# Hybrid encoder layer on one core: branch B's copies of h tied to the projections, its outputs in DRAM by halves of 512 tokens, the low parts of h's sums on VectorE, and branch A's scores of the prompt in runs of four blocks

## The chip, the cores and the metric

One core of a Trainium2 chip runs the whole kernel. The metric is the device time of one execution in microseconds (us); times of single instructions are also in us unless marked ns. The engines are called as in the profile: PE (TensorE, matmuls), PEld (its weight loads), DVE (VectorE), ACT (ScalarE), POOL (GpSimd) and SP (SyncE, which issues all DMAs of this kernel).

## The reference

One encoder layer with shared weights is applied to two batches, a prompt of 512 tokens and a sample of 1024, each of width 1024. All is fp32. Cut to what matters:

```
h = rmsnorm(x, norm_g)
qa, ka, va, za, qb, kb, vb, zb, ga, gb = split(h @ w_in)
oa = neighbourhood_attention(rmsnorm(qa), rmsnorm(ka), va, rpb) * silu(za)   # 8 heads of 64
ob = window_gqa_attention(rmsnorm(qb), rmsnorm(kb), vb, t5, sink) * silu(zb) # 8 heads, 2 of k and v
merged = sigmoid(ga) * (oa @ w_o_a) + sigmoid(gb) * (ob @ w_o_b)
y = x + merged @ w_out
```

Branch A sees the tokens as a grid 64 wide and attends to a window of 8 rows by 16 columns. Branch B attends to tokens at most 128 away; four query heads share one head of k and v.

## The kernel before, in words

Every fp32 matrix is held as two parts, hi and lo, and a product of two matrices is three matmuls: hi·hi, lo·hi and hi·lo. So h lives as `hh` and `hl`, a weight as `whi` and `wlo`, and so on. `split` (L1168) makes the parts of a tile: hi by a rounding copy on ACT (L1172), lo as the difference on DVE or POOL (L1177).

Each batch goes through two phases.

**Attention** (`attention_phase`, L651) works on six groups: A0 to A3 with two heads each, then B0 and B1 with four query heads each. In a group, each tile of 128 tokens is projected (`project`, 24 matmuls at L764 into one of two PSUM banks tagged p). The norm of q and k follows: squares (ACT L783), their sums `ss` (DVE L788), `rs_v` and its power `rs_r` (POOL L795 and L802), and the scaled `qk` (DVE L819), which PE transposes (L864). When the tiles that a block of queries needs are there, `attend` (L911) issues its scores: matmuls with half the rows (L937), for two heads side by side in the array, three for each head, into PSUM banks tagged x (there are five). `weigh` (L961) takes a block's scores on: bias and minimum on DVE (L972), exponential on ACT (L981), the reciprocal of the sums (DVE L1005), scaling on POOL (L1011) or DVE (L1013), transposes on PE (L1029), split of the result `pp` (ACT L1035, DVE L1040), products with v (L1066), and the output `ot` is stored to DRAM by SP (A: L1090, B: L1102). In the prompt the blocks of branch A are taken two at a time, each head with a bank of its own. Between these, "fill" products of the later gate projections use bank d.

Branch B reads h with its tokens in another order, so `project` first copies tiles of `hh` and `hl` into `hb` (L665 on ACT, L667 on DVE). A copy may start once its part of h is there.

**The dense phase** (`dense_phase`, L1139) computes the paths z and g, the merge and the output. Pairs of weight blocks go through one level of Strassen's scheme (`pair_strassen`, L1349), which wants sums S of weight blocks (L1166) and sums T of blocks of h. The sample's four sums T are kept in DRAM, `t_d`, and read back by `stored_sums` (L1236, loads L1245), each in four tiles that are split; their buffers on the way are called U, fh and w. Weights arrive as `raw` (L1257), and `weight_tiles` (L1260) splits them. The matmuls are L1293 to L1295. `post_z` (L1524) takes a finished z tile: it loads the attention output (`ot<-o_d`, L1535; for branch B two loads, even and odd heads, which DVE adds as `ot<-ot`), multiplies (`C<-C,ot`), and stores to `u_d` (L1520).

**The order.** No order is written down by hand. `Flow` (L141 on) plans the whole program before it is built: each operation has a priority, the engines that may do it with a cost on each, and what it must follow. An operation with two engines goes to the one that the plan has free earlier; a rule named `port` keeps two such operations from standing on DVE and POOL at once. Each engine then runs its own list in order. So a change of one operation can move others on all engines.

Of the kernel before, what the change touches and what calls it, by code (L numbers as in the profile page):

```python
# [25 lines left out]
FILL_P, FILL_S = 3, 8  # L26
SLACK = 1.1
SCRATCH = 1024
CLASSIC_P = (4, 8, 4)
# [325 lines left out]
def encoder_kernel(  # L355
# [47 lines left out]
    t_d = dpool.tile([4, 4, P, NT_S // 2], F32, tag="t_d", name="t_d")  # L403
    o_d = {geo.nt: dpool.tile([2, 8, P, geo.nt], F32, tag=f"o_d{geo.nt}", name=f"o_d{geo.nt}") for geo in (gp, gs)}

# [245 lines left out]
    def attention_phase(geo, hh, hl, h_ops, mask_d, early, late):  # L651
# [79 lines left out]
        def project(br, w, t, prio):  # L731
# [179 lines left out]
        def attend(br, gi, g, batch, nb_t, info, prio):  # L911

            nh = 2 if br == "A" else 4
            k0 = 2 * (gi % 2)
            states = []
            for block in batch:
                sums = tuple(tile_([P, 4], F32, tag, 3) for tag in ("mx", "sm", "rs", "es"))
                pss = [bank("x") for _ in range(nh)]
                sbs = [tile_([P, GW], F32, "sb", 8 if nt == NT_S else 9) for _ in range(nh)]
                states.append((block, sums, pss, sbs))  # L920
# [5 lines left out]
            def emit(e):  # L926

                for block, _, pss, _ in states:
                    runs, tiles, width, step, whole = places(block)
                    q = queries(block)  # L930
                    for pair in range(nh // 2):
                        at = runs[0][0] if whole else pair * P
                        for n, (u, k) in enumerate(((0, 0), (0, 1), (1, 0))):
                            for i in range(2):
                                rows = slice(64 * i, 64 * i + 64)
                                kv = kt.t[rows, k0 + k].rearrange("p (t n) -> p t n", n=P)
                                pe.matmul(  # L937
                                    pss[2 * pair + i].t[:, :width], q.t[rows, u, at : at + P],
                                    kv[:, tiles[0] : tiles[-1] + 1 : step], start=n == 0, stop=n == 2,
                                )  # L940

            def queries(block):
# [4 lines left out]
            o = f.op(  # L947
                (("pe", ns),), emit, prio, new=[v for _, _, pss, sbs in states for v in (*pss, *sbs)],
                use=[queries(block) for block in batch], after=[o for b in batch for t in b[1] for o in info[t][2]],
# [11 lines left out]
        def weigh(br, gi, g, block, sums, pss, sbs, nb_t, info, prio):  # L961
# [6 lines left out]

            def score(i, ps, sb):
                def emit(e, i=i, ps=ps, sb=sb):  # L970
                    init = 3.0e38 if br == "A" else nsink[:, 4 * g + i : 4 * g + i + 1]
                    dve.tensor_tensor_reduce(  # L972
                        out=sb.t[:, :width], in0=ps.t[:, :width], in1=bias_of(br, nb_t, i, table), scale=1.0,
                        scalar=init, op0=ALU.add, op1=ALU.min, accum_out=mx.t[:, i : i + 1],
# [16 lines left out]

            for i, (ps, sb) in enumerate(zip(pss, sbs)):
                score(i, ps, sb)
            if br == "B":
# [81 lines left out]
            if br == "A":  # L1076
# [10 lines left out]
                def emit():  # L1087
                    if len(runs) == 1:
                        dst = over(o_d[nt][0, g], runs).rearrange("(i p) n -> p i n", i=2)
                        nc.sync.dma_start(dst, ot.t[:64, ::2])  # L1090
                        return
                    for i in range(2):
                        dst = over(o_d[nt][0, g, 64 * i : 64 * i + 64], runs)
                        nc.sync.dma_start(dst, ot.t[:64, 2 * i].rearrange("p (a b) -> p a b", b=64))

                stores[g, runs[0][0] // 512].append(sp(emit, 65536, prio, use=[ot]))
            else:
                for e in range(2):
                    dst = o_d[nt][e, 4 + 2 * g : 6 + 2 * g, :, runs[0][0] : runs[0][0] + P]
                    dst = dst.rearrange("c (i d) n -> d (c i) n", d=64)  # L1100
                    o = sp(
                        lambda e=e, dst=dst: nc.sync.dma_start(dst, ot.t[e * 64 : e * 64 + 64]),  # L1102
                        131072, prio, use=[ot],
                    )
                    for c in (4 + 2 * g, 5 + 2 * g):
                        for n in range(nt // 512):
                            stores[c, n].append(o)

        f.slack = SLACK
        groups = [("A", 0), ("A", 1), ("A", 2), ("A", 3), ("B", 0), ("B", 1)]  # L1110
        for gi, (br, g) in enumerate(groups):
# [14 lines left out]
            for t in range(nb):  # L1126
# [12 lines left out]
    def dense_phase(geo, hh, hl, h_ops, o_stores, exps_done, start, opened, tp, up, p0, p1, p2, x_t, y_t, classic, fill, after_gates=None, side=None):  # L1139
# [27 lines left out]

        def split(hi, lo, src, n, prio, new_hi, new_lo, src_v, after=()):  # L1168

# [5 lines left out]
            b = f.op(  # L1175
                any_tt(n),
                lambda e: engines[e].tensor_tensor(lo(), src(), hi().bitcast(F32), op=ALU.subtract), prio,  # L1177
# [58 lines left out]
        def stored_sums(prio, d, after):  # L1236

            tv, ops = {}, {}
            for j in (1, 2, 0, 3):
                tv[j] = tuple(f.value(tp, [P, 4, nh], F32R, "T", 8) for _ in range(2))  # L1240
                vh, vl = tv[j]
                for k in range(4):
# [6 lines left out]
                        lambda vh=vh, k=k: vh.t[:, k], lambda vl=vl, k=k: vl.t[:, k], lambda st=st: st.t[:, :nh], nh, prio,  # L1249
                        (vh, k == 0), (vl, k == 0), [st],  # L1250
                    )
# [7 lines left out]

        def weight_tiles(operands, per, prio):  # L1260

# [4 lines left out]
            for i, src in enumerate(operands):  # L1266
                at, q = [], 0
                while q < 4:
# [6 lines left out]
                        lambda src=src, sc=sc: src.t[:, sc], m * P, prio,  # L1275
                        (hi, ti not in seen), (lo, ti not in seen), [src],
                    )
# [71 lines left out]
        def pair_strassen(srcs, post, prio, mov_h, mov_t, seed=None, last=False, kept=None):  # L1349
# [10 lines left out]
            first = [] if kept else [raw[0, 0], raw[0, 1]]  # L1360
            w = weight_tiles([*first, s2, s3, s1, raw[1, 1], s4], 6, prio - 0.5)
            w = [None] * (7 - len(w)) + w
# [161 lines left out]
        def post_z(c, a, n, v, in_psum, prio):  # L1524
# [3 lines left out]
            for e, ot in enumerate(ots):  # L1528
                if c < 4:
                    src, dst = o_d[nt][e, c, :, a : a + n], lambda ot=ot: ot.t[:, :n]  # L1530
                else:
                    src = o_d[nt][e, c].rearrange("p (i n) -> p i n", n=P)[:, :, a // nb : a // nb + m]
                    dst = lambda ot=ot: ot.t[:, :n].rearrange("p (i n) -> p i n", n=m)
                dma(
                    lambda dst=dst, src=src: nc.sync.dma_start(dst(), src), 512 * n, prio - 0.5, new=[ot],  # L1535
                    after=o_stores[c, a // nh],
# [417 lines left out]
```

## Time and profile before

| | us |
|---|---|
| median of three runs | 1136.02 |
| lowest and highest run | 1134.59, 1136.24 |
| the profiled execution | 1135.29 |
| its span | 1133.5 |
| PE busy in it | 1119.0 |

The page and the views tell of one profiled execution, 1135.29 us, of which 1133.5 us are the span from the first to the last instruction. PE's granted clock was 1.00. The stages, by the windows view: the prompt's attention runs from about 30 to 220 us, its dense phase to 404, the sample's attention to about 797 and its dense phase to the end. In that view PE is busy for all of 30 to 404; it lacks 2.6 us of 161 in 404 to 565, 0.2 of 232 in 565 to 797, 2.5 of 31 in 797 to 828, and 2.7 of 305 after that. A row of a timeline reads: start, duration, engine, line and operation, output<-inputs, shapes, how many; in brackets the idle time before it and what ended that. The durations of matmuls are modelled and overlap, so PE's pace is read from start to start.

### The profile page before, as it was taken

What the parts mean: (1) busy time and instruction counts of PE and PEld (TensorE: products, weight loads), DVE (VectorE), ACT (ScalarE), POOL (GpSimd) and SP (SyncE); (2) the same over time, 40 slices, a digit from 0 to 9 for tenths busy, and PEclk for the clock granted to TensorE, in tenths of its full rate; (3) what the DMA queues carried; (4) which work ended last, traced back from release to release, by engine and by line L of the source; (5) the groups of instructions that cost most, each with busy time, mean ns of one, the idle gap of its engine ahead of it and who ended that gap; (6) DMA issues with size and microseconds to landing.
All of it is one profiled execution on the core that took longest, in us unless ns stands there. A gap on an engine that the chain in (4) does not pass through costs nothing.

```text
span 1133.5 us, 18690 instructions
## 1 busy us (share of the span) xinstructions
PE 1119.0 (99%) x6079; PEld 973.2 (86%) x6079; DVE 860.1 (76%) x1988; ACT 651.9 (58%) x1499; POOL 337.3 (30%) x438
## 2 busy tenths in 40 slices
PE   8999999999999999999999999999999999999998
PEld 6999988888888889999999988988788888888887
DVE  5888797587776568787878888885988766677764
ACT  6777987644432257565769888876543335423430
POOL 4653433000011154434324344420333322222211
PEclk9999999999999999999999999999999999999999
DMA  7854543488886732121212314244977645867862
GB/s 263 276 155 138 184 115 103 110 257 248 256 278 216 254 128 91 27 63 30 82 41 85 81 38 112 57 131 121 307 241 234 224 156 170 281 207 222 280 215 93
DMA packets 139108, 186.11 MB, mean 164 GB/s; under 512 B 29897, under 2 KB 68561, under 8 KB 139010
## 3 DMA queue, kind: packets, MB, share of 16 engines
q1 hardware_dynamic: 139010, 184.91, 51.8%
q8 instruction: 48, 0.79, 0.3%
q14 instruction: 50, 0.41, 0.1%
HBM read 137.66 MB, written 51.92 MB: 167 GB/s over the span
## 4 chain that ended last, share of the span: by engine, by line
PE 93%; DMA 2%; DVE 2%; issue 1%; ACT 1%; POOL 1%; SPq 0%; DVEq 0%; ACTq 0%
PE p L764 25%; PE x L1294 9%; PE x L1295 9%; PE x L1293 9%; PE x L1066 5%; PE x L937 5%; PE x L1029 5%; PE d L1293 4%; PE d L1295 4%; PE d L1294 4%; PE p L1294 4%; PE p L1295 4%; PE p L1293 4%; PE x L864 2%; DMA w<-in_w_att_dram 1%
## 5 line engine op out<-in xcount | busy, mean ns | idle before, releaser
L764 PE MATMUL p<-whi,hh 128*128 128x384 f32 x384 | 133.4, 348 | 0.0
L764 PE MATMUL p<-whi,hl 128*128 128x384 f32 x384 | 132.2, 344 | 0.0
L764 PE MATMUL p<-wlo,hh 128*128 128x384 f32 x384 | 131.8, 343 | 0.0
L1172 ACT ACTIVATE whi<-raw 128x512 fp32r<-128x512 f32 (+1 forms) x140 | 81.4, 600 | 71.2 <-PE x L1294 22.3
L981 ACT ACTIVATE sb<-sb,mx 128x384 f32<-128x384 f32 (+1 forms) x192 | 107.8, 565 | 16.9 <-DVE mx L972 16.5
L1295 PE MATMUL x<-T,wlo 128*128 128x512 f32 x280 | 108.9, 389 | 0.0
L1294 PE MATMUL x<-T,whi 128*128 128x512 f32 x280 | 108.9, 389 | 0.0
L1293 PE MATMUL x<-T,whi 128*128 128x512 f32 x280 | 108.9, 389 | 0.0
L764 PE MATMUL p<-whi,hb 128*128 128x384 f32 x384 | 107.6, 346 | 0.0
L1177 POOL TENSOR_TENSOR wlo<-raw,whi 128x512 fp32r<-128x512 f32 (+1 forms) x33 | 39.5, 1204 | 215.6 <-DMA raw<-in_w_g_dram 112.9
L1040 DVE TENSOR_TENSOR pp<-x,pp 128x512 fp32r<-128x512 f32 (+1 forms) x136 | 82.5, 638 | 19.6 <-ACT pp L1035 19.0
L1177 DVE TENSOR_TENSOR wlo<-raw,whi 128x512 fp32r<-128x512 f32 (+1 forms) x107 | 72.0, 682 | 32.3 <-ACT whi L1172 28.7
L802 POOL TENSOR_TENSOR rs_r<-rs_v,mhalf 128x4 f32<-128x4 f32 (+1 forms) x72 | 80.5, 1118 | 5.7
L1035 ACT ACTIVATE pp<-x 128x512 fp32r<-128x512 f32 (+1 forms) x136 | 70.8, 559 | 15.8 <-PE x L1029 14.3
L1294 PE MATMUL x<-hl,whi 128*128 128x512 f32 x200 | 77.8, 389 | 0.0
L1295 PE MATMUL x<-hh,wlo 128*128 128x512 f32 x200 | 77.8, 389 | 0.0
L1293 PE MATMUL x<-hh,whi 128*128 128x512 f32 x200 | 77.8, 389 | 0.0
L1066 PE MATMUL x<-pp,v 128*128 128x256 f32 (+1 forms) x368 | 75.8, 322 | 0.0
L764 PEld LDWEIGHTS p<-whi,hl 128*128 128x128 f32 x384 | 72.6, 189 | 1.3 <-issue 1.0
L764 PEld LDWEIGHTS p<-wlo,hh 128*128 128x128 f32 x384 | 72.7, 189 | 1.0 <-issue 0.7
L764 PEld LDWEIGHTS p<-whi,hh 128*128 128x128 f32 x384 | 72.7, 189 | 0.7 <-DVE v L812 0.3
L764 PEld LDWEIGHTS p<-whi,hb 128*128 128x128 f32 x384 | 69.1, 188 | 3.1 <-issue 1.3
(388 smaller groups left out, 2965.1 us busy)
## 6 DMA issues: line engine op xcount, KB each, us to landing
raw<-in_w_g_dram SPq DMA_DIRECT2D x84, 256.0 KB
w<-in_w_att_dram SPq DMA_DIRECT2D x46, 384.0 KB
raw<-in_w_z_dram SPq DMA_DIRECT2D x40, 256.0 KB
ot<-o_d SPq DMA_DIRECT2D x36, 256.0 KB
g_d<-C SPq DMA_DIRECT2D x34, 256.0 KB
fr<-in_w_g_dram SPq DMA_DIRECT2D x28, 256.0 KB
raw<-in_w_out_dram SPq DMA_DIRECT2D x28, 256.0 KB
out_dram<-C SPq DMA_DIRECT2D x19, 256.0 KB
```

The lines of the kernel that those rows point to most:

```text
L764: pe.matmul(ps.t[:, :GW], part[u](k), mv.t[:, c], start=k == 0 and m == 0, stop=k == KC - 1 and m == 2,)
L802: lambda e: nc.gpsimd.tensor_tensor(r.t[:, :nn], rv.t[:, :nn], mhalf[:, :nn], op=ALU.pow),
L937: pe.matmul(pss[2 * pair + i].t[:, :width], q.t[rows, u, at : at + P], kv[:, tiles[0] : tiles[-1] + 1 : step], start=n == 0, stop=n == 2,)
L981: act.activation(sb.t[:, :width], sb.t[:, :width], AF.Exp, bias=mx.t[:, i : i + 1], scale=-1.0, accum_out=sm.t[:, i : i + 1],)
L1035: lambda e, pt=pt, pp=pp, nn=nn: act.activation(pp.t[:, 0, :nn], pt.t[:, :nn], AF.Copy),
L1040: lambda e, pt=pt, pp=pp, nn=nn: dve.tensor_tensor(pp.t[:, 1, :nn], pt.t[:, :nn], pp.t[:, 0, :nn].bitcast(F32), op=ALU.subtract),
L1066: pe.matmul(out(), v.t[:, vs], mv(), start=first, stop=last)
L1172: (("act", ACT_(n)),), lambda e: act.activation(hi(), src(), AF.Copy), prio,
L1177: lambda e: engines[e].tensor_tensor(lo(), src(), hi().bitcast(F32), op=ALU.subtract), prio,
L1293: pe.matmul(out, hi.t[:, cs], mh(), start=first and k == 0, stop=False, **more)
L1294: pe.matmul(out, hi.t[:, cs], ml(), start=False, stop=False, **more)
L1295: pe.matmul(out, lo.t[:, cs], mh(), start=False, stop=last and k == len(ws) - 1, **more)
```

## The change

There are four edits.

1. A branch B copy now also waits until the projection of six tiles earlier has begun (`AHEAD = 6`; `f.begun` holds the first operation of each projection).
2. Branch B's outputs have a DRAM tensor of their own, `ob_d`, by halves of 512 tokens, with the tokens in the order in which branch B makes them. A sample block's output was stored by two DMAs in pieces of 512 B (one for the even and one for the odd heads); now by two, one for each half, in pieces of 256 B. A prompt block needs one DMA instead of two. `post_z` read branch B's part as 8 pieces of 256 B on each of 128 partitions (sample); now as one line of 2 KB on each.
3. `split` has a new argument `both`. The low parts of the sums T from `t_d`, and of the weight tiles of pair 0, can be made on DVE only; POOL is no longer offered.
4. In the prompt's branch A four blocks go through `attend` together, and two blocks share a PSUM bank: the second writes its scores from column 256 on.

```
+AHEAD = 6
...
-    o_d = {geo.nt: dpool.tile([2, 8, P, geo.nt], ...
+    o_d = {geo.nt: dpool.tile([4, P, geo.nt], ...
+    ob_d = {geo.nt: dpool.tile([geo.nt // 512, 8, P, 512], ...
...
-    prio - 1, new=[hb[m][q]], hold=[v], after=[o for u in h_ops.values() for o in u], port=True,
+    prio - 1, new=[hb[m][q]], hold=[v], port=True,
+    after=[*(o for u in h_ops.values() for o in u), f.begun[nt, prio - AHEAD]],
...
+    shared = br == "A" and nt == NT_P
...
-    pss = [bank("x") for _ in range(nh)]
+    second = shared and len(states) % 2
+    pss = [(v, 256) for v, _ in states[-1][2]] if second else [(bank("x"), 0) for _ in range(nh)]
...
-    for e in range(2):
-        dst = o_d[nt][e, 4 + 2 * g : 6 + 2 * g, :, runs[0][0] : runs[0][0] + P]
-        dst = dst.rearrange("c (i d) n -> d (c i) n", d=64)
+    m, t = 512 // nb, runs[0][0] // P
+    for n in range(nt // 512):
+        dst = ob_d[nt][n, 4 * g : 4 * g + 4, :, t * m : t * m + m].rearrange("a p m -> p a m")
...
-    size = 2 if br == "A" else 1
+    size = 1 if br == "B" else 4 if nt == NT_P else 2
...
-    any_tt(n),
+    any_tt(n)[: 1 + both],
...
+    (vh, k == 0), (vl, k == 0), [st], both=d is m_d,
...
+    w = weight_tiles([*first, s2, s3, s1, raw[1, 1], s4], 6, prio - 0.5, prio > 0)
...
-    src = o_d[nt][e, c].rearrange("p (i n) -> p i n", n=P)[:, :, a // nb : a // nb + m]
+    src = ob_d[nt][a // nh, 2 * c - 8 : 2 * c - 6, e * 64 : e * 64 + 64, :n]
```

The planner makes a new order of it. Three places follow, first the program of before, then the changed one; lines of the changed file are 2 to 6 higher. PE's matmuls are as many as before; in the prompt's attention their order is new, from 220 to 564 us it is the same, and in the sample it differs only near 564 to 646 and 797 to 828.

The first place is the first scores of the prompt's branch A. On PE, before (`kt` and `qt` are the transposed k and q, `d` a fill bank):

```order
L1294 MATMUL d<-hl,fh 128x512
L1295 MATMUL d<-hh,fl 128x512
L764 MATMUL p<-wlo,hh 128x384
L937 MATMUL x<-kt,qt 128x256 x12
L864 MATMUL x<-ident,qk 128x128 x2
L764 MATMUL p<-whi,hl 128x384
```

and of the change:

```order
L767 MATMUL p<-whi,hl 128x384 x2
L767 MATMUL p<-whi,hh 128x384
L767 MATMUL p<-wlo,hh 128x384
L943 MATMUL x<-kt,qt 128x256 x24
L767 MATMUL p<-whi,hl 128x384
```

Two runs of 12 have become one of 24. On DVE behind it, in the changed program (the two rows `sb,mx` and `mx` are one score operation; five of the eight stand up to the end of the second row):

```order
L978 ISA sb,mx<-x,bias 128x256
L978 ISA mx 128x1
L822 TENSOR_TENSOR qk<-p,rs_r 128x256
L1011 RECIPROCAL rs<-sm 128x2
L978 ISA sb,mx<-x,bias 128x256
L978 ISA mx 128x1
L1011 RECIPROCAL rs<-sm 128x2
```

A block's reciprocal stands between the scores of later blocks; before, it stood behind the four scores of its pair of blocks.

The second place is on DVE at the start of the sample's attention, at 402 to 406 us of the profile before. Of before:

```order
L788 TENSOR_REDUCE ss<-sq 128x4
L812 TENSOR_TENSOR v<-p,v 128x2x64
L667 CAST hb<-hl 128x512 x2
L788 TENSOR_REDUCE ss<-sq 128x4
L819 TENSOR_TENSOR qk<-p,rs_r 128x256
```

and of the change:

```order
L791 TENSOR_REDUCE ss<-sq 128x4
L815 TENSOR_TENSOR v<-p,v 128x2x64
L791 TENSOR_REDUCE ss<-sq 128x4
L822 TENSOR_TENSOR qk<-p,rs_r 128x256
L815 TENSOR_TENSOR v<-p,v 128x2x64
```

The two copies stand further down, in the group A3; two on ACT have left the place in the same way.

The third place is on DVE in the sample's z path, one set of four tiles of T (U, fh, U, w), at 808 to 813 us of the profile before. Of before, where the tile from fh is POOL's:

```order
L1177 TENSOR_TENSOR T<-U,T 128x512
L1177 TENSOR_TENSOR wlo<-S,whi 128x256
L1166 TENSOR_TENSOR U<-fr,x 128x512
L1177 TENSOR_TENSOR T<-U,T 128x512
L1166 TENSOR_TENSOR ot<-ot 128x512
L1177 TENSOR_TENSOR T<-w_10666,T 128x512
L1166 TENSOR_TENSOR C<-C,ot 128x512
```

and of the change:

```order
L1181 TENSOR_TENSOR T<-U,T 128x512
L1170 TENSOR_TENSOR U<-fr,x 128x512
L1181 TENSOR_TENSOR T<-fh,T 128x512
L1181 TENSOR_TENSOR T<-U,T 128x512
L1181 TENSOR_TENSOR T<-w_10645,T 128x512
L1170 TENSOR_TENSOR U<-U,x 128x512
L1170 TENSOR_TENSOR ot<-ot 128x512
```

The set's four tiles now stand on DVE with `ot<-ot` behind them. POOL, which had the tile from fh and one `C<-C,ot`, has sums of weights (`S<-raw,S`) and more of the splits `wlo<-S` in their stead.

More of the change, by code (lines that the diff above doesn't have):

```diff
@@ L403, in encoder_kernel @@
     t_d = dpool.tile([4, 4, P, NT_S // 2], F32, tag="t_d", name="t_d")
-    o_d = {geo.nt: dpool.tile([2, 8, P, geo.nt], F32, tag=f"o_d{geo.nt}", name=f"o_d{geo.nt}") for geo in (gp, gs)}
+    o_d = {geo.nt: dpool.tile([4, P, geo.nt], F32, tag=f"o_d{geo.nt}", name=f"o_d{geo.nt}") for geo in (gp, gs)}
+    ob_d = {geo.nt: dpool.tile([geo.nt // 512, 8, P, 512], F32, tag=f"ob_d{geo.nt}", name=f"ob_d{geo.nt}") for geo in (gp, gs)}
     s_d = dpool.tile([4, 4, P, 512], F32, tag="s_d", name="s_d")
@@ L936, in emit @@
                                 kv = kt.t[rows, k0 + k].rearrange("p (t n) -> p t n", n=P)
+                                ps, a = pss[2 * pair + i]
                                 pe.matmul(
-                                    pss[2 * pair + i].t[:, :width], q.t[rows, u, at : at + P],
+                                    ps.t[:, a : a + width], q.t[rows, u, at : at + P],
                                     kv[:, tiles[0] : tiles[-1] + 1 : step], start=n == 0, stop=n == 2,
@@ L947, in attend @@
             o = f.op(
-                (("pe", ns),), emit, prio, new=[v for _, _, pss, sbs in states for v in (*pss, *sbs)],
+                (("pe", ns),), emit, prio, new=[v for _, _, pss, sbs in states for v in (*(ps for ps, a in pss if not a), *sbs)],
                 use=[queries(block) for block in batch], after=[o for b in batch for t in b[1] for o in info[t][2]],
@@ L967, in weigh, with score, emit @@
             mx, sm, rs, es = sums
-            def score(i, ps, sb):
-                def emit(e, i=i, ps=ps, sb=sb):
+            def score(i, ps, a, sb):
+                def emit(e, i=i, ps=ps, a=a, sb=sb):
                     init = 3.0e38 if br == "A" else nsink[:, 4 * g + i : 4 * g + i + 1]
                     dve.tensor_tensor_reduce(
-                        out=sb.t[:, :width], in0=ps.t[:, :width], in1=bias_of(br, nb_t, i, table), scale=1.0,
+                        out=sb.t[:, :width], in0=ps.t[:, a : a + width], in1=bias_of(br, nb_t, i, table), scale=1.0,
                         scalar=init, op0=ALU.add, op1=ALU.min, accum_out=mx.t[:, i : i + 1],
@@ L990, in score @@
                 x.vals = [*x.vals, mx]
-            for i, (ps, sb) in enumerate(zip(pss, sbs)):
-                score(i, ps, sb)
+            for i, ((ps, a), sb) in enumerate(zip(pss, sbs)):
+                score(i, ps, a, sb)
             if br == "B":
@@ L1088, in emit @@
                     if len(runs) == 1:
-                        dst = over(o_d[nt][0, g], runs).rearrange("(i p) n -> p i n", i=2)
+                        dst = over(o_d[nt][g], runs).rearrange("(i p) n -> p i n", i=2)
                         nc.sync.dma_start(dst, ot.t[:64, ::2])
@@ L1092, in emit @@
                     for i in range(2):
-                        dst = over(o_d[nt][0, g, 64 * i : 64 * i + 64], runs)
+                        dst = over(o_d[nt][g, 64 * i : 64 * i + 64], runs)
                         nc.sync.dma_start(dst, ot.t[:64, 2 * i].rearrange("p (a b) -> p a b", b=64))
@@ L1097, in weigh @@
             else:
-                for e in range(2):
-                    dst = o_d[nt][e, 4 + 2 * g : 6 + 2 * g, :, runs[0][0] : runs[0][0] + P]
-                    dst = dst.rearrange("c (i d) n -> d (c i) n", d=64)
+                m, t = 512 // nb, runs[0][0] // P
+                for n in range(nt // 512):
+                    dst = ob_d[nt][n, 4 * g : 4 * g + 4, :, t * m : t * m + m].rearrange("a p m -> p a m")
                     o = sp(
-                        lambda e=e, dst=dst: nc.sync.dma_start(dst, ot.t[e * 64 : e * 64 + 64]),
-                        131072, prio, use=[ot],
+                        lambda n=n, dst=dst: nc.sync.dma_start(dst, ot.t[:, :, n * m : n * m + m]), 2048 * m, prio, use=[ot],
                     )
                     for c in (4 + 2 * g, 5 + 2 * g):
-                        for n in range(nt // 512):
-                            stores[c, n].append(o)
+                        stores[c, n].append(o)
         f.slack = SLACK
@@ L1166, in tt, with split @@
             return f.op(choice, lambda e: engines[e].tensor_tensor(out(), in0(), in1(), op=op), prio, **kw)
-        def split(hi, lo, src, n, prio, new_hi, new_lo, src_v, after=()):
+        def split(hi, lo, src, n, prio, new_hi, new_lo, src_v, after=(), both=True):
             kw = lambda v, new: {"hold": [v]} if new is None else {"new": [v]} if new else {"into": [v]}
@@ L1258, in load_raw, with weight_tiles @@
             return v
-        def weight_tiles(operands, per, prio):
+        def weight_tiles(operands, per, prio, both=True):
             n = -(-len(operands) * 4 // per)
@@ L1275, in weight_tiles @@
                         lambda src=src, sc=sc: src.t[:, sc], m * P, prio,
-                        (hi, ti not in seen), (lo, ti not in seen), [src],
+                        (hi, ti not in seen), (lo, ti not in seen), [src], both=both,
                     )
@@ L1529, in post_z @@
                 if c < 4:
-                    src, dst = o_d[nt][e, c, :, a : a + n], lambda ot=ot: ot.t[:, :n]
+                    src = o_d[nt][c, :, a : a + n]
                 else:
-                    src = o_d[nt][e, c].rearrange("p (i n) -> p i n", n=P)[:, :, a // nb : a // nb + m]
-                    dst = lambda ot=ot: ot.t[:, :n].rearrange("p (i n) -> p i n", n=m)
+                    src = ob_d[nt][a // nh, 2 * c - 8 : 2 * c - 6, e * 64 : e * 64 + 64, :n]
                 dma(
-                    lambda dst=dst, src=src: nc.sync.dma_start(dst(), src), 512 * n, prio - 0.5, new=[ot],
+                    lambda ot=ot, src=src: nc.sync.dma_start(ot.t[:, :n], src), 512 * n, prio - 0.5, new=[ot],
                     after=o_stores[c, a // nh],
```

2 lines of the change are left out of this document (removed).

## The prediction

> **What bounds the kernel now.** I began with the head of the profile's page: the span, the busy times, and the split of the chain that ended last.
>
> ```profile
> span 1133.5 us, 18690 instructions
> PE 1119.0 (99%) x6079; PEld 973.2 (86%) x6079; DVE 860.1 (76%) x1988; ACT 651.9 (58%) x1499; POOL 337.3 (30%) x438
> PE 93%; DMA 2%; DVE 2%; issue 1%; ACT 1%; POOL 1%; SPq 0%; DVEq 0%; ACTq 0%
> ```
>
> TensorE (PE) is busy 99% of the span and carries 93% of the chain. So a change can pay in two ways only: cheaper PE work, or fewer of the places at which PE waits. The second view, PE's waits, lists those places.
>
> ```profile
> PE x L864 <- DVE qk L819: 3.1, 3, 1.8
> PE d L1294 <- DVE T L1177: 1.6, 1, 1.6
> PE p L1294 <- DVE T L1177: 0.9, 2, 0.7
> ```
>
> Columns: total us, times, longest. Apart from the program's start, which the change doesn't touch, three waits are for qk (the normed q and k, which PE transposes), and three for T, the low halves of h's sums, in the z phase of the sample batch. Score waits, or waits for a branch B copy or an attention output, do not appear: these can act only through what they delay. The change issues as many matmuls as before, so its whole worth lies in the cost of switching between kinds of matmul, in the wait at 404 us, and in the z phase at 809 to 821 us; its risk lies in what the new order makes late.
>
> **Part 1: score runs of 24 in place of 12.** PE's timeline at one run of the prompt's branch A:
>
> ```profile
> 57.75 0.63 PE L1066 MATMUL x<-pp,v 128*128 128x256 f32 x4
> 58.22 0.38 PE L864 MATMUL x<-ident,qk 128*128 128x128 f32 x2
> ...
> 63.43 0.34 PE L764 MATMUL p<-whi,hl 128*128 128x384 f32 x1
> 63.60 0.34 PE L764 MATMUL p<-whi,hh 128*128 128x384 f32 x1
> 63.87 0.97 PE L937 MATMUL x<-kt,qt 64*128 64x256 f32 x12
> 64.78 0.45 PE L764 MATMUL p<-wlo,hh 128*128 128x384 f32 x1
> ```
>
> The ends of matmuls are modelled, so I count from start to start. Full-height matmuls of 256 columns take (58.22 − 57.75) / 4 = 0.1175 each. The run holds 12 matmuls of half the rows, in pairs that share the array: 6 × 0.1175 = 0.705. From its start to the next matmul it takes 64.78 − 63.87 = 0.91, so 0.205 is the way out. The way in is read before it: from 63.60 to 63.87 the last projection takes 0.27, where one ahead of a projection takes 63.60 − 63.43 = 0.17: another 0.10. One run costs about 0.30 beyond its work. Eight runs become four: −1.2; ends −0.8 and −1.4, since the new neighbours of a run may differ. The sum takes −1.2.
>
> The cover that this needs: the longer run makes eight score operations at once instead of four. The rows of the chain behind a run (DVE adds the bias, ACT takes the exponential, POOL or DVE scales, PE transposes):
>
> ```profile
> 66.25 0.42 DVE L972 CUSTOM_DVE_ANT_0 sb<-x,bias 128x256 f32<-128x256 f32 x1
> 66.60 0.42 DVE L972 CUSTOM_DVE_ANT_0 sb<-x,bias 128x256 f32<-128x256 f32 x1
> ...
> 66.74 0.49 ACT L981 ACTIVATE sb<-sb,mx 128x256 f32<-128x256 f32 x1
> 67.23 0.49 ACT L981 ACTIVATE sb<-sb,mx 128x256 f32<-128x256 f32 x1
> ...
> 69.33 1.18 POOL L1011 TENSOR_TENSOR sb<-sb,rs 128x256 f32<-128x256 f32 x2 [0.56 <-DVE rs L1005]
> 69.62 0.60 PE L1029 MATMUL x<-ident,sb 128*128 128x128 f32 x4
> ```
>
> A score takes 0.35 of DVE (66.25 to 66.60), an exponential 0.49 of ACT, two scalings 1.18 of POOL. In the changed order the first block's reciprocal stands on DVE behind five scores and a qk as wide as a score, then come two scalings on POOL. From the run's start that is 1.6 (24 matmuls: 12 × 0.1175 + 0.2) + 6 × 0.35 + 0.2 for the reciprocal (an estimate) + 1.2 = 5.1, or 5.7 if it waits for one more exponential and a crossing between engines. The first transposes stand on PE behind 20 projections of 0.17, three products of 512 columns (twice 0.1175 each) and two transposes: 1.6 + 3.4 + 0.7 + 0.4 = 6.1. So 0.4 or more is left over. The second block's transposes come four transposes and five projections later (0.4 + 0.9), its scalings 1.2 later: 0.5 is left over. That is thin, and the four groups are planned alike. I put +0.1 per group, +0.4 in all, between 0 and +2.5 (the longest wait on a qk, 1.8, once, and 0.2 in the other three). Not below nothing: no wait stands there that could go.
>
> **Part 2: branch B's copies of h later.** POOL, DVE and PE at the longest wait for qk:
>
> ```profile
> 402.23 1.31 POOL L1177 TENSOR_TENSOR fl<-fr,fh 128x512 fp32r<-128x512 f32 x1 [11.40 <-ACT fh L1172]
> 403.62 1.22 POOL L795 TENSOR_SCALAR rs_v<-ss 128x4 f32<-128x4 f32 x1
> 404.92 1.01 POOL L802 TENSOR_TENSOR rs_r<-rs_v,mhalf 128x4 f32<-128x4 f32 x1
> 406.02 0.19 POOL L795 TENSOR_SCALAR rs_v<-ss 128x4 f32<-128x4 f32 x1
> ...
> 402.62 2.15 DVE L667 CAST hb<-hl 128x512 fp32r<-128x512 f32 x2
> 405.97 0.42 DVE L819 TENSOR_TENSOR qk<-p,rs_r 128x256 f32<-128x256 f32 x1 [0.75 <-POOL rs_r L802]
> ...
> 404.21 0.40 PE L1295 MATMUL d<-hh,fl 128*128 128x512 f32 x1
> 406.45 0.44 PE L864 MATMUL x<-ident,qk 128*128 128x128 f32 x2 [1.84 <-DVE qk L819]
> ```
>
> PE goes from 404.21 to 406.45, 2.24, where such a product takes 0.23: 2.0 lost. The chain is rs_v, rs_r, qk. The rs_v of 4 values took 1.22 while DVE ran two hb copies, and 0.19 when DVE ran none. In the changed order these copies are gone from this place on DVE and on ACT; nothing else in the rows around it moves. The chain is then shorter by 1.03. POOL's fl, 1.31 ahead of rs_v, stays, and rs_v can't start before 403.54. So −1.0 of the 2.0; the ends are 0 (if POOL is held by something else) and −2.0 (if fl, too, was stretched by the copies). The copies come back in the sample's fourth branch A group, where PE waits for nothing now; the worst price is the same collision there, +1.0; I take 0, since the list has no wait there now that a copy could lengthen.
>
> **Part 3: outputs of B by halves, and splits on DVE.** The windows of the z phase's two stretches, cut at 797.19; the columns are us, then each engine's busy time with its count, PE's clock, the DMA share, GB/s:
>
> ```profile
> 786.31:797.19 10.88, 10.88 (x49) 9.01 (x48) 6.57 (x12) 8.68 (x17) 0.00 (x0) 1.00 0.91 276
> 797.19:828.04 30.85, 28.37 (x121) 22.21 (x120) 29.14 (x41) 14.71 (x30) 10.71 (x7) 1.00 0.82 258
> ```
>
> 48 products in 10.88 are 0.2267 each; the next 120 should take 27.2 and take 30.85: 3.65 lost at full clock. The DMA share shows how full the memory queues are, and DVE is busy 29.14 of 30.85. The rows around the longest wait:
>
> ```profile
> 806.77 0.68 DVE L1177 TENSOR_TENSOR T<-U,T 128x512 fp32r<-128x512 f32 x1
> 810.10 1.25 DVE L1166 TENSOR_TENSOR ot<-ot 128x512 f32<-128x512 f32 x1 [0.46 <-DMA ot<-o_d]
> 811.27 1.75 DVE L1177 TENSOR_TENSOR T<-w,T 128x512 fp32r<-128x512 f32 x1
> ...
> 809.05 1.75 POOL L1177 TENSOR_TENSOR wlo<-S,whi 128x512 fp32r<-128x512 f32 x1
> 810.76 1.71 POOL L1177 TENSOR_TENSOR wlo<-raw,whi 128x512 fp32r<-128x512 f32 x1
> ...
> 811.11 0.40 PE L1293 MATMUL d<-T,whi 128*128 128x512 f32 x1
> 813.08 0.50 PE L1294 MATMUL d<-T,whi 128*128 128x512 f32 x1 [1.57 <-DVE T L1177]
> ```
>
> T<-w is due at 811.3 and ends at 813.0. Three things made it late: it stands on DVE behind ot<-ot, which waited 0.46 for its DMA; that ran 1.25 and T<-w itself 1.75 beside POOL's splits, where a free one takes 0.68. In the changed order T<-w stands ahead of ot<-ot. That removes 0.46 + 1.25 = 1.7 from in front of it, all of this wait (1.97 − 0.23 = 1.74 from start to start). The two waits for T in bank p (0.9 by the list) and the restarts make up the rest, 3.65 − 1.74 = 1.9. SP's rows:
>
> ```profile
> 803.14 1.41 SPq L1535 DMA_DIRECT2D ot<-o_d  x2
> 804.60 3.58 SPq L1520 DMA_DIRECT2D u_d<-C  x1
> ...
> 814.42 0.42 SPq L1520 DMA_DIRECT2D u_d<-C  x1
> ```
>
> A store behind two loads of B's output took 3.58 to issue, against 0.42: 3.2 in which SP issues no t_d load. The loads are 1024 pieces of 256 B each; afterwards 128 lines of 2 KB, so I expect most of these 3.2 to go, and the t_d loads to come earlier.
>
> What stays: the order gives T<-fh and one C<-C,ot to DVE, and gives POOL other sums and splits of weights for them. A POOL operation of 1.3 to 1.7 can stretch a T by 1.07 (1.75 − 0.68) as before. So of the 3.65 I take the 1.74 that the order settles as gone, and of the remaining 1.9 a third, 0.65. That is −2.4; the ends are 0 (the first rival) and −3.65.
>
> The cost side, B's stores:
>
> ```profile
> 785.75 1.24 SPq L1102 DMA_DIRECT2D o_d<-ot__10494  x2
> L1094 SPq DMA_DIRECT2D o_d<-ot__2184 x2: 622/623/624, 141.8 to 142.5; - x2
> ```
>
> They remain two per sample block, but in 256-B pieces in place of 512-B. Branch A's stores in the prompt with 256-B pieces (second row) take 0.62 each to issue, as B's do now (1.24 for two). So nothing is added on SP. In the prompt two stores become one, off the path. I take 0, and at worst the 0.7 of one more such store ahead of the first t_d load.
>
> A rule speaks against this: the Trainium skill, DMA: Bandwidth & Descriptors, "Specifications", gives 512 B as the least for full rate, below which the engine reads, modifies and writes. By it the stores would cost more DMA time in the sample's attention; nothing waits for them before the z phase, so by it the sum would stay the same. No run so far shows its price.
>
> **The sum.** −1.2 + 0.4 − 1.0 − 2.4 = −4.2. The profiled execution took 1135.29 (span 1133.5 and 1.8 around it), so 1131.1 against it; it lies 0.73 below the median of the three runs, 1136.02, which the result is measured like: **1131.8**.
>
> **Rivals.**
> 1. The z wait only moves: POOL's new sums collide with T at other places, and DVE, 29.14 of 30.85 busy, gets one T and one multiply more (1.36). For it: the thin slack of DVE. Against: T stands ahead of its multiply now, and slow stores go. Then −1.2 − 1.0 + 0.4 = −1.8: **1134.2**, chance 0.18. The Trainium skill, SBUF — State Buffer, section "SBUF: two separate sides", says that a VectorE operation with two SBUF inputs and a GpSimd operation that reads SBUF lock each other out for a whole instruction, whichever starts first; by that rule every operation that POOL is given beside a T costs that T its full time, and the sum would be this rival's. The 1.75 of T<-w against 0.68 agrees.
> 2. Slower: the burst of four blocks. If the first transposes of a group wait until all eight exponentials are done instead of the first four, each of the four groups loses 4 × 0.49 = 1.96, less the 0.4 left over, and its last products with v as much again where bank x is held (5 banks, four of them filled by the run): 1.56 + 1.56 to 1.56 + 1.96 per group, 12 to 14 in all, with the rest kept: 1136.0 − 4.6 + 13 = **1144**. It decides from 1.7 per group (6.9 in all, which takes −4.6 past +2.3). For: eight scores are 2.8 of DVE in a row. Against: the order puts reciprocals between the scores, and scalings before the last exponentials. Chance 0.08.
> 3. All of it: fl was stretched too, and no T waits. −1.2 − 2.0 − 3.65 = −6.9: **1129.2**, chance 0.14.
> 4. The change doesn't do what it says: the planner spends the freed time elsewhere and new waits of 2 to 4 us open: **1136**, chance 0.05.
>
> **Numbers.** The forecast has the remaining 0.55 and its own range, 1130.4 (z gives 3.65, switches 1.4) to 1133.5 (z gives 1.2, the prompt's attention loses 0.9). The range 1129.0 to 1135.2 takes in rivals 1 and 3. Under 0.2% (2.3 us, what a measurement can tell from no change) lie rival 4 and most of rival 1: same 0.20, faster 0.55 + 0.14 + 0.03 = 0.72, slower 0.08.
>
> **What would show it.** Right: four runs of 24 in the prompt; rs_v near 0.2 at the place of 403.62 and half the qk wait left; no store of u_d over 1 us behind two ot loads; T waits under 1.3 in sum. Wrong: waits for sb or pp in the prompt (rival 2), T waits of over 2 (rival 1), or a wait for qk over 1 in the sample's fourth branch A group.

## The result, and the profile after

The changed kernel is slower, and by far: a median of 1226.24 us (1224.84 to 1227.59) against 1135.3, a ratio of 1.0804 with a 95% interval of 1.0787 to 1.0821. The forecast was 1131.8, with a range of 1129.0 to 1135.2. The profiled execution took 1226.16, its span is 1224.4.

The head of the page of the changed kernel: the span, the busy times, and two rows of the span in 40 slices of 30.6 us (busy tenths of PE, and PE's granted clock in tenths).

```profile
span 1224.4 us, 18692 instructions
PE 1146.8 (94%) x6079; PEld 986.7 (81%) x6079; DVE 852.7 (70%) x1963; ACT 652.0 (53%) x1502; POOL 351.5 (29%) x460
PE   8999999966998999999999999997894599999998
PEclk9999999987998999999999999998897699999999
```

The count of matmuls is the same, 6079. The span grew by 90.9. PE was busy 27.8 longer (1146.8 against 1119.0) for the same matmuls, and stood idle 63.1 longer. Both happen mainly in two places, slices 9 to 10 (245 to 306 us) and 28 to 32 (826 to 980): the stretches in which `post_z` loads branch B's output, in the prompt and in the sample. There PE's clock is down too. Slice 13 (367 to 398), in the prompt's merge, is down to 8 in both rows; the experiments come back to it. Before, both rows showed 9 at all these places.

PE's waits (total, times, longest), and DVE's longest in total:

```profile
PE x L1299 <- DVE wlo L1181: 29.6, 6, 9.9
PE x L1297 <- ACT whi L1176: 11.9, 2, 10.1
PE p L1299 <- DVE wlo L1181: 8.4, 2, 6.6
PE x L1297 <- ACT T L1176: 4.9, 1, 4.9
PE x L1297 <- ACT hh L1176: 3.6, 2, 3.1
PE p L1297 <- ACT T L1176: 3.5, 1, 3.5
PE x L867 <- DVE qk L822: 2.7, 3, 1.2
PE d L1298 <- DVE T L1181: 1.2, 3, 0.7
...
DVE ot L1170 <- DMA ot<-ob_d: 90.2, 11, 11.4
```

The long waits are new. Most are for weights that DVE and ACT should have split; two, of 4.9 and 3.5, are for the high part of T, which ACT makes. The waits for qk and, in bank d, for the low part of T did not grow. DVE itself waits 90.2 us for loads of branch B's output. One of the long ones step by step, first SP and DVE, then PE:

```profile
235.20 1.19 SPq L1538 DMA_DIRECT2D ot<-ob_d  x2
248.88 2.10 SPq L1538 DMA_DIRECT2D ot<-ob_d  x2
...
248.16 0.69 DVE L1170 TENSOR_TENSOR ot<-ot 128x512 f32<-128x512 f32 x1 [9.19 <-DMA ot<-ob_d]
261.62 0.69 DVE L1170 TENSOR_TENSOR ot<-ot 128x512 f32<-128x512 f32 x1 [6.92 <-DMA ot<-ob_d]
263.78 0.68 DVE L1181 TENSOR_TENSOR wlo<-raw,whi 128x512 fp32r<-128x512 f32 x1
...
257.58 0.39 PE L1298 MATMUL p<-hl,whi 128*128 128x512 f32 x1
264.52 0.80 PE L1299 MATMUL p<-hh,wlo 128*128 128x512 f32 x1 [6.55 <-DVE wlo L1181]
265.11 0.63 PE L1297 MATMUL p<-hh,whi 128*128 128x512 f32 x1
265.54 0.63 PE L1298 MATMUL p<-hl,whi 128*128 128x512 f32 x1
```

Two loads of B's output are issued at 235.20, and DVE can add them only at 248.16, 13 us later. The next pair is issued at 248.88 and added at 261.62, 12.7 later. DVE runs its list in order: behind this second `ot<-ot` stand the multiply and then `wlo<-raw` (263.78), the low part of a weight that PE needs at 257.8. PE gets it at 264.5. The windows view shows what the loads did while nothing else ran on the DMA engines, and what came after the wait (the last three columns are PE's clock, the DMA share and GB/s):

```profile
242.50:247.90 5.40, 5.40 (x26) 4.46 (x25) 0.00 (x0) 0.00 (x0) 0.00 (x0) 1.00 0.13 51
264.50:268.90 4.40, 4.38 (x10) 3.47 (x11) 2.97 (x5) 1.61 (x4) 0.00 (x0) 0.51 0.40 118
```

The share of 0.13 is 2/16: as much as two DMA engines at work all the time, and they move 51 GB/s. A load is 128 × 512 × 4 bytes = 262 KB, so 5.1 us at that rate, and a pair 10.3, on the same two engines. And after the 6.6 us of idle time PE ran at half its clock: 0.43 from start to start (265.11 to 265.54) where 0.23 is usual.

What makes it two engines can be read in the diff. The source of a load is `ob_d[..., 2 * c - 8 : 2 * c - 6, e * 64 : e * 64 + 64, :n]`: two heads, of each 64 rows of 2 KB, with other rows between the two blocks. So the access pattern has an outermost dimension of 2. Before, it was 128 (the partitions). The Trainium skill, DMA: Bandwidth & Descriptors, section "Why a DMA increments its semaphore by 16 and not by 1", says that the number of DMA engines is the largest up to 16 that divides the slowest dimension of both access patterns. By that rule it is 2 here, and the trace's 0.13 agrees.

### The profile page after: what moved, and what is told of

It is laid out like the page before. It is cut to its first block, busy times and chain, and to the rows that moved or that the text cites. A ratio compares the mean times of both kernels' runs of the same rounds, so it can differ in the third digit from the quotient of the medians.

```text
span 1224.4 us, 18692 instructions
## 1 busy us (share of the span) xinstructions
PE 1146.8 (94%) x6079; PEld 986.7 (81%) x6079; DVE 852.7 (70%) x1963; ACT 652.0 (53%) x1502; POOL 351.5 (29%) x460
## 5 line engine op out<-in xcount | busy, mean ns | idle before, releaser
L1299 PE MATMUL x<-T,wlo 128*128 128x512 f32 x280 | 113.5, 405 | 16.9 <-DVE wlo L1181 16.7
L1297 PE MATMUL x<-T,whi 128*128 128x512 f32 x280 | 113.0, 403 | 16.7 <-ACT whi L1176 11.9
L1181 POOL TENSOR_TENSOR wlo<-raw,whi 128x512 fp32r<-128x512 f32 (+1 forms) x35 | 42.5, 1219 | 253.3 <-ACT whi L1176 253.1
L1298 PE MATMUL x<-T,whi 128*128 128x512 f32 x280 | 112.5, 402 | 1.1 <-DVE T L1181 1.1
L1299 PE MATMUL x<-hh,wlo 128*128 128x512 f32 x200 | 80.8, 404 | 12.9 <-DVE wlo L1181 12.9
L1297 PE MATMUL x<-hh,whi 128*128 128x512 f32 x200 | 80.5, 402 | 3.7 <-ACT hh L1176 3.6
L1298 PE MATMUL x<-hl,whi 128*128 128x512 f32 x200 | 80.3, 402 | 0.8 <-DVE hl L1181 0.8
L1299 PEld LDWEIGHTS x<-T,wlo 128*128 128x128 f32 x280 | 54.5, 195 | 31.8 <-DVE wlo L1181 18.9
L1297 PEld LDWEIGHTS x<-T,whi 128*128 128x128 f32 x280 | 54.7, 195 | 29.1 <-ACT whi L1176 12.7
L1517 ACT ACTIVATE C<-C 128x512 f32<-128x512 f32 x38 | 23.8, 631 | 99.9 <-DVE C L1170 78.2
```

The source lines that it names most:

```text
L1297: pe.matmul(out, hi.t[:, cs], mh(), start=first and k == 0, stop=False, **more)
L1298: pe.matmul(out, hi.t[:, cs], ml(), start=False, stop=False, **more)
L1299: pe.matmul(out, lo.t[:, cs], mh(), start=False, stop=last and k == len(ws) - 1, **more)
L1517: (("act", ACT_(n)),), lambda e: act.activation(sg.t[:, :n], v.t[:, :n], fn), prio,
```

## The experiments

**Theory A**: the loads run on 2 of 16 engines because their outermost dimension is 2, and nearly all of the loss comes from that. **Rival B**: the new order, with splits of T on DVE and other work on POOL. **Rival C**: the 256-B stores, or the place of the data in DRAM, make the reads slow.

### rows and cols: the changed kernel, each load in two

`rows` cuts a load between the two heads, so that each DMA has 64 rows as its outermost dimension; `cols` cuts it by columns, and the 2 stays outermost.

```
 rows:  for i in range(2):
            nc.sync.dma_start(ot.t[64 * i : 64 * i + 64, :n], src[i])
 cols:  for i in range(2):
            nc.sync.dma_start(ot.t[:, n // 2 * i : n // 2 * i + n // 2], src[:, :, n // 2 * i : n // 2 * i + n // 2])
```

> The changed kernel with one edit: each load of branch B's output, whose DRAM side is [2 heads x 64 rows x 2 KB], goes out as two DMAs of [64 rows x 2 KB]. The order of all engines is that of the changed kernel; the bytes, the pieces of 2 KB and their addresses are the same. Theory A (the load runs on 2 of the 16 DMA engines because its outermost dimension is 2: the trace shows a DMA share of 0.13 = 2/16 while nothing else runs, about 24 packets per us of 84 ns): the loads spread, the 90 us of PE waits and slow-clock matmuls go, and what is left of the change shows: 1128 to 1136 us, DMA share far over 0.13 at those places. Rival B (the new order: sums and splits given to POOL, T's splits on VectorE): no difference, 1220 to 1230. Rival C (256-B stores or the place of the data in DRAM makes the reads slow): 1215 to 1230.

> Control for the kernel above: each load is also cut into two DMAs, but by columns, [2 heads x 64 rows x 1 KB] each, so the outermost dimension stays 2. Theory A: both halves run on the same 2 engines, 1220 to 1245 us (1-KB pieces may cost more each). If the mere number of DMAs in flight is what helps, it falls to the time of the kernel cut by rows. Rivals B and C: 1215 to 1235.

Measured: `rows` 1141.29 us (ratio to before 1.0056, 1.0037 to 1.0075), which is over the 1128 to 1136 that I had expected, and `cols` 1233.57 (a single run). The order of every engine is the same in both, and the bytes are too. B and C, which have no use for the way of cutting, fall, and so does the mere number of DMAs, which `cols` has as well. In `rows` the first pair of loads reaches DVE 5.5 us after the issue (235.31 to 240.86) in place of 13.0, and the DMA share is 0.71 from 237.0 to 240.9; in `cols` it takes 14.1 (236.48 to 250.54). DVE's waits for these loads come to 9.2 us in `rows` and 88.6 in `cols`, against 90.2 in the changed kernel and 7.7 before. `rows`:

```profile
235.31 2.42 SPq L1542 DMA_DIRECT2D ot<-ob_d  x4
...
240.86 0.69 DVE L1170 TENSOR_TENSOR ot<-ot 128x512 f32<-128x512 f32 x1 [1.74 <-DMA ot<-ob_d]
```

So 85 of the 91 us come from the loads that run on two engines. But `rows`, which is the change without this fault, is still 6 us slower than before and not 4 faster: other steps of the forecast failed too.

### only_ob and no_ob: the layout alone, and all without it

`only_ob` is the kernel before with the new layout and undivided loads; `no_ob` is the changed kernel with the layout of before.

> The kernel before with part 2 of the change alone (B's outputs in DRAM by halves, loads undivided). Theory A: 12 pairs of loads, each about 11 us on 2 engines, with some 7 us of PE lost for each: 1200 to 1235 us. Rival B (order, parts 1, 3, 4): about 1132 to 1137.

> The changed kernel with B's outputs stored and loaded as before, so parts 1, 3 and 4 alone. Theory A: the loss is gone, 1130 to 1136 us (the forecast's -1.2 for score runs, +0.4, -1.0 at 404 us, and a part of the z phase). Rival B: 1215 to 1230.

Measured: `only_ob` 1230.79 (a single run), `no_ob` 1141.68 (1.0059, 1.0042 to 1.0077). The layout alone makes a loss as large as that of the whole change. And `no_ob`, like `rows`, is 6 us slower: I had expected 1130 to 1136, so this was a miss.

### p1, p3, p4 and only_ob_rows: one part at a time

Each is the kernel before with one part of the change: `p1` the later copies, `p3` `both`, `p4` the runs of four blocks, `only_ob_rows` the layout with loads cut as in `rows`. The edits are those of the diff.

> The kernel before with part 1 alone (branch B's copies wait for the projection six tiles earlier). My forecast for this part was -1.0 at 404 us; rows and no_ob (all parts, with quick loads of B) showed -0.3 and -1.4 there, and yet 6 us more in sum. Theory D (each part by itself is worth what its place shows): 1134 to 1135, the wait for qk at 404 us down by about 1. Theory E (the 6 us come from the new plan of the prompt's attention, which this part alone makes too): 1138 to 1143, with a stall of PE in the prompt's merge at 350 to 360 us.

> The kernel before with part 3 alone (low parts of T and of pair 0's weights on VectorE only). Its order differs from before in the sample's z path alone. My forecast for the z path was -2.4, in rows and no_ob the stretch from the last product with v to the end took +2.1 and +3.1. If part 3 is the cause (POOL gets sums and splits of weights that stretch T by 1.07 each): 1137 to 1139, the waits for T at 800 to 830 us over 4 in sum. If it is not: 1132.5 to 1135.5.

> The kernel before with part 4 alone (four blocks at once in the prompt's branch A). Score runs -0.75 (15.90 to 15.15 in rows and no_ob) and transposes of qk -0.2; against that the waits of fill products for the copy fc, +1.0 in rows and no_ob. Theory D: 1135 to 1136. Theory E (the new plan shifts PE against DVE so that the prompt's merge stalls for 3 to 7 us): 1138 to 1142.

> The kernel before with part 2 alone, and each load of B's output cut into two DMAs of 64 rows so that it spreads. PE's order is that of before. If B's loads in pieces of 256 B were what held the z path up (3.2 us of a store's issue): 1132 to 1134, no store of u_d over 1 us behind them, the T waits of 808 to 821 us smaller. If the transfers were hidden: 1134.5 to 1136. The pair rows against no_ob, whose PE order is the same, gave no difference (1141.3 and 1141.7).

| kernel | median us | ratio, 95% interval |
|---|---|---|
| p1 | 1138.40 | 1.0038, 1.0024 to 1.0053 |
| p3 | 1138.93 | 1.0033, 1.0018 to 1.0047 |
| p4 | 1139.86 | 1.0049, 1.0030 to 1.0069 |
| only_ob_rows | 1140.69 | 1.0057, 1.0039 to 1.0074 |

Every part by itself is slower, by 0.3 to 0.6%. Theory D, that each is worth what its place shows, fails for all of them, and the loss of `p3` is in the range (1137 to 1139) that blamed part 3. Alone they lose 3.5, 4.0, 4.9 and 5.8 us, 18 in sum, and `rows`, which has all four, loses 6: what a part costs alone is not what it costs in the whole. What the profiles, one of each kernel, show:

`p1`: rs_v takes 0.20 at the place of 404 us, as forecast, and PE's wait there is 1.06 in place of 1.84, but the next qk is waited for as well, 0.51:

```profile
407.01 0.44 PE L866 MATMUL x<-ident,qk 128*128 128x128 f32 x2 [1.06 <-DVE qk L821]
409.53 0.44 PE L866 MATMUL x<-ident,qk 128*128 128x128 f32 x2 [0.51 <-DVE qk L821]
```

There is no stall at 350 to 360 us. So the time is as theory E had it (1138 to 1143), but its mechanism is not in this profile.

`p3`: the waits for T grew, as the forecast's first rival had it. PE's waits, then a T beside a split on POOL:

```profile
PE d L1294 <- DVE T L1177: 2.1, 4, 0.7
PE p L1294 <- DVE T L1177: 1.4, 2, 0.7
...
812.52 1.77 DVE L1177 TENSOR_TENSOR T<-U,T 128x512 fp32r<-128x512 f32 x1
...
812.02 1.73 POOL L1177 TENSOR_TENSOR wlo<-raw,whi 128x512 fp32r<-128x512 f32 x1
```

3.5 us in six waits, against 2.5 in three before; this T costs 1.77 in place of 0.68 while POOL works. (My figure of over 4 was too high.) The split that POOL no longer gets was replaced on POOL by other work, and that hits T just the same.

`p4`: qk is late at two more places of the prompt's attention. PE's waits, the two new ones, and POOL ahead of each:

```profile
PE x L864 <- DVE qk L819: 5.9, 5, 1.8
...
65.09 0.44 PE L864 MATMUL x<-ident,qk 128*128 128x128 f32 x2 [1.80 <-DVE qk L819]
...
71.62 1.69 PE L940 MATMUL x<-kt,qt 64*128 64x256 f32 x24
73.23 0.44 PE L764 MATMUL p<-wlo,hh 128*128 128x384 f32 x1
75.56 0.44 PE L864 MATMUL x<-ident,qk 128*128 128x128 f32 x2 [1.54 <-DVE qk L819]
...
60.52 2.03 POOL L1180 TENSOR_TENSOR fl<-fr,fh 128x512 fp32r<-128x512 f32 x1
73.77 0.19 POOL L467 TENSOR_SCALAR nv<-ns 128x1 f32<-128x1 f32 x1 [1.59 <-ACT junk L463]
```

Two new waits of 1.8 and 1.5, 5.9 in all against 3.1. What holds qk up is POOL's list in the new plan, and directly ahead of these waits it has no score work: the first time rs_v and rs_r stand behind an `fl` of 2.03, the second time rs_r stands behind `nv`, a step of the norm of x that waits 1.59 for ACT. POOL had been busy without a break since 46.98, behind the first burst, so the burst may have a share in the first wait; that is not shown. The time is as theory E had it (1138 to 1142), but again without the stall in the merge. The run of 24 itself takes 73.23 − 71.62 = 1.61, against twice 0.91 before, so 0.2 are saved each time.

`only_ob_rows`: I had expected 1136 at most, so this was a miss too. PE's order is that of before, and yet there is a new wait, in the prompt's merge (L1293 of before):

```profile
PE x L1292 <- ACT hh L1171: 3.1, 1, 3.1
```

The waits for T fell from 2.5 to 1.4 in sum, but 3.1 of waiting came up in the prompt. The next kernels take the halves apart.

### rows_s, rows_p and em_s: the layout by batch

`rows_s` and `rows_p` are `only_ob_rows` for the sample or the prompt alone. `em_s` is the sample alone with even and odd heads' parts apart in DRAM, so that one undivided DMA has 128 rows outermost:

```
+    ob_d = {... dpool.tile([geo.nt // 512, 2, 8, 64, 512], ...
+    src = ob_d[nt][a // nh, e, 2 * c - 8 : 2 * c - 6, :, :n].rearrange("c d n -> (c d) n")
```

> The kernel before with part 2 for the sample alone, loads cut into two DMAs of 64 rows. The order of PE, DVE, ACT and POOL is that of before; on SP each of the 16 sample loads of B's output is two DMAs. With part 2 for both batches the stretch from the last product with v to the end was 1.3 shorter than before, and the prompt's dense phase 6.4 longer. Theory F (the prompt's half of part 2 makes that stall, the sample's half is a gain): 1133 to 1134.5, the waits for T at 808 to 821 us under 2.5 in sum, the prompt as before. Rival G (any edit of the DMAs tips the prompt's merge into its stall): 1137 to 1141.

> The kernel before with part 2 for the prompt alone, loads cut into two DMAs of 64 rows. PE's and POOL's order is that of before; on DVE and SP the sample's norm, whose tiles are loaded and scaled during the prompt's z path, moves. Theory F: 1138 to 1142, PE waits 3 to 6 us at 353 to 362. Rival G: the same, and then rows_s too. If the prompt's half is free: 1134.5 to 1136.

> The kernel before with a layout for the sample alone in which even and odd heads' parts lie apart, so that a load is 128 rows of 2 KB one behind the other, in one DMA; a sample block is stored by four DMAs of 64 partitions. If the outermost dimension is what decides (128 here, 2 in the changed kernel), these loads are as quick as those cut in two: a DMA share far over 0.13, no stall of PE over 2 us: 1133 to 1138 (the four stores move the order of the z path a little). If 2-KB lines from this tensor were slow in themselves: over 1170 (16 of the 24 slow loads).

Measured: `rows_s` 1134.28 us (0.9993, 0.9979 to 1.0008), `rows_p` 1138.76 (1.0036, 1.0019 to 1.0052), `em_s` 1132.71 (0.9985, 0.9970 to 0.9999). Theory F holds for the stall: the prompt's half makes it, the sample's half does not. That the sample's half is a gain is not shown; `rows_s` cannot be told from the kernel before. `em_s` is the quickest, 2 us below the kernel before, but its interval only just leaves out 1. Its loads are whole, with 2-KB lines from a new tensor like the changed kernel's, and quick (DVE waits for them twice, 0.9 us in sum): they have an outermost dimension of 128 in place of 2.

SP in `rows_s`, at the second of the two places where a store took 3.66 and 3.58 to issue before:

```profile
800.62 2.37 SPq L1552 DMA_DIRECT2D ot<-ob_d  x4
803.04 0.58 SPq L1531 DMA_DIRECT2D u_d<-C  x1
```

The stores issue in 0.44 and 0.58, as forecast, but the four issues of loads ahead of them take 2.4 to 3.2 in place of 1.4 to 2.1. In `em_s` two loads take 0.97 to issue (796.63) and the waits for T are gone from PE's list; the stretch from 794 to 829 us has PE busy for all of it. The loads need not be the reason alone, since the order of its z path is new as well (the tile T from fh that POOL makes at 807.79 before stands on DVE, at 806.98).

```profile
794.00:829.00 35.00, 35.00 (x156) 28.86 (x155) 32.90 (x53) 20.33 (x42) 9.66 (x6) 1.00 0.84 293
```

PE in `rows_p`, in the prompt's merge, and the same `hh<-C` on ACT ahead of it, first before, then in `rows_p`:

```profile
357.10 0.40 PE L1306 MATMUL x<-hh,wlo 128*128 128x512 f32 x1
360.62 0.50 PE L1304 MATMUL x<-hh,whi 128*128 128x512 f32 x1 [3.12 <-ACT hh L1183]
361.34 0.79 PE L1305 MATMUL x<-hl,whi 128*128 128x512 f32 x1 [0.22 <-DVE hl L1188]
361.93 0.63 PE L1306 MATMUL x<-hh,wlo 128*128 128x512 f32 x1
362.36 0.63 PE L1304 MATMUL x<-hh,whi 128*128 128x512 f32 x1
...
344.23 0.63 ACT L1172 ACTIVATE hh<-C 128x512 fp32r<-128x512 f32 x1 [1.42 <-DVE C L1166]
...
350.61 0.63 ACT L1183 ACTIVATE hh<-C 128x512 fp32r<-128x512 f32 x1 [1.36 <-DVE C L1177]
```

A wait of 3.1, and behind it some nine matmuls at half clock, 0.43 each: 3.3 + 0.5 + 9 × 0.2 = 5.6 us. The profile of before has no wait at this place. The `hh<-C` comes 6.4 later than before where PE is 1.3 later, so the chain on SP, DVE and ACT has lost 5 us against PE. The orders of SP, DVE and ACT differ from those of before in the z path, at 226 to 312 us, where the plan moved the loads of the sample's norm and their work; that this is what made the chain late is argued.

**What stays open.** The stall in the merge stands in the profile of each of the six kernels that have part 2 in the prompt (the changed one, `rows`, `cols`, `only_ob`, `only_ob_rows`, `rows_p`) and in none of the others. It does not account for the rest of the loss. `no_ob`, `p1` and `p4` have runs of 1143.12, 1141.54 and 1141.45 us with a mean granted clock of 1.000, so nothing like the half clock behind that stall was in them; 10 of the 12 runs of `rows_p` have 0.997 to 0.999. The profiled executions of these three kernels were their shortest runs (1137.83, 1136.66 and 1136.71), so where the others lost some 5 us more was not seen. `p3` changes nothing ahead of the sample's z path; of the 4.3 us by which its span is longer, 2.3 are in that path, and most of the others come at 372 to 411 us, in waits at places that it leaves as they were. Such waits come and go from one profile to the next. Whether a new plan costs some us whatever the edit was not tested by itself.

## Why the prediction was wrong

**The step that failed** stands in part 3: "The loads are 1024 pieces of 256 B each; afterwards 128 lines of 2 KB, so I expect most of these 3.2 to go, and the t_d loads to come earlier." I priced a load by its pieces and its bytes. Its shape, which sets how many DMA engines share it, I did not look at; the diff shows it, and the rule cited above stands in the page of the Trainium skill from which I took another. The bound was missing too: I gave the loads no price above nothing, and no rival was about them. The measured price is 13 us for a pair in place of 5.5, 12 pairs, 85 us in all. And that stores which issue quickly would bring T forward failed as well (the z path, below).

**Why it was not hidden.** I held that a load acts only through what it delays, which is right; I did not ask what is queued behind `ot<-ot` on DVE. In the wait shown above it is the split of the next weights (263.78), for which PE then stood still.

**Score runs, −1.2.** Right in size: from start to next matmul the eight runs took 7.29 in sum, the four of `p4` take 6.52, and there are four ways in less, of 0.1 each.

**New waits in the prompt's attention, +0.4 between 0 and +2.5.** The size is within the bounds in the changed kernel, but from another cause: fill products wait for the copy of bank d, 1.3 in place of 0.2, and no wait for qk over 0.5 stands in the prompt. So it is in `rows`:

```profile
PE d L1297 <- ACT fc L1623: 1.2, 3, 0.7
```

In `p4` alone the two new waits for qk make 3.3, over the bound. My check followed one burst's own chain (scores to transposes) and missed the fill bank and the next tile's qk.

**The wait at 404 us, −1.0.** The step on POOL is right: rs_v takes 0.19 or 0.20 in the changed kernel, `rows`, `no_ob` and `p1`, against 1.22 before. PE's gain is not shown. In `no_ob` the wait is 0.48, in `rows`, with the same order on PE, DVE, ACT and POOL, 1.59:

```profile
402.85 0.20 POOL L797 TENSOR_SCALAR rs_v<-ss 128x4 f32<-128x4 f32 x1
404.66 0.44 PE L866 MATMUL x<-ident,qk 128*128 128x128 f32 x2 [0.48 <-DVE qk L821]
...
411.91 0.44 PE L867 MATMUL x<-ident,qk 128*128 128x128 f32 x2 [1.59 <-DVE qk L822]
```

`p1` has 1.06 and the changed kernel 1.24. Kernels without part 1 have from 0.70 (`rows_p`) to 1.98 (`em_s`) at this place, against 1.84 before. `p1` and `no_ob` also wait for the next qk (0.51 and 0.70), as `rows_p` does (1.01). One profile of each does not tell −1.0 from no gain.

**The z path, −2.4.** Wrong in sign. The 120 products took 30.85 before (797.20 to 828.05). With part 3 and loads that are not slow they take 33.18 (`p3`), 32.97 (`rows`) and 33.90 (`no_ob`), so 2 to 3 us more: the 1.74 that I took as settled by the order came back as waits for T in other places, beside other work on POOL. That was my first rival, at 0.18. The rest, by way of the stores, does not hold either. In `rows` the stores issue in 0.33 and 0.47, and the waits for T are 3.3 in sum; in `rows_p`, which has the sample's layout and orders of before, they take 3.19 and 3.77, and the waits for T are 0.9:

```profile
811.08 3.77 SPq L1531 DMA_DIRECT2D u_d<-C  x1
...
819.39 0.50 PE L1305 MATMUL d<-T,whi 128*128 128x512 f32 x1 [0.90 <-DVE T L1188]
```

The stretch takes 28.85 there and 28.75 in `rows_s`, so that the layout's share of it is not shown; only `em_s`, at 27.24, reaches full pace.

**What no case had.** The prompt's dense phase runs with little in hand: in `rows_p` a chain on SP, DVE and ACT that is some 5 us behind costs PE 5 to 6 us in the merge, and nothing on PE's waits list before tells of it.

## What to carry to other kernels

For each DMA that a change rewrites, write down the outermost dimension of both sides before its bytes: 2 there means two engines, however long the lines are. A load that nobody waits for in the profile is priced by what stands behind its first user on that engine's list. And a waits list of before shows what is late, not what is nearly late: where a stage has no waits but a busy DMA queue, give every edit of its loads a bound on the bad side. Last, a wait of one profile is not yet a wait of the kernel: waits of up to 1.6 us came and went here at places that an edit had left as they were.

## What the runs showed of the hardware that I had not expected

A wait of PE can cost more than its length. After 1.84 us idle, at 404 us before, the next matmuls ran at full pace; after 3.1 (`rows_p`) and 6.6 (the changed kernel) some ten matmuls ran at 0.43 in place of 0.23, for about 4 us, with a granted clock of 0.59 (360.6 to 364.8) and 0.51 (264.5 to 268.9). That is 2 us on top of each of these two waits; in the changed kernel PE was busy 27.8 us longer in all. But the length of a single wait does not decide it. In `no_ob` two short waits close together were followed by the same half pace, with a clock of 0.76 from 809 to 816:

```profile
809.74 0.50 PE L1299 MATMUL d<-T,whi 128*128 128x512 f32 x1 [1.24 <-DVE T L1182]
...
811.43 0.80 PE L1299 MATMUL d<-T,whi 128*128 128x512 f32 x1 [0.73 <-DVE T L1182]
812.02 0.63 PE L1300 MATMUL d<-T,wlo 128*128 128x512 f32 x1
812.45 0.63 PE L1298 MATMUL d<-T,whi 128*128 128x512 f32 x1
```

The Trainium skill, TensorE: Matmul & The Clock Gate, section "Part 1: The HAM clock gate (the "warmup" mystery)", tells of half the clock after an idle window of about 3.4 us, and of as long a busy time until it is back. The runs agree roughly on how long the half clock lasts; as for its start the runs decide: 3.1 was enough, and in `no_ob` 1.24 and 0.73.
